# Hybrid RWKV-7 / GLA / SSD stack on one core: more output columns open at once at the head of a layer, and a new pace table for the modulation loads

## The chip, the cores and the metric

One Trainium2 chip, one of its cores. The metric is the device time of one execution of the whole program in microseconds (us), the median over runs. Smaller is better.

## The reference

Four layers on a sequence of 256 tokens of width 2048, batch 1, in float32: layer 0 is RWKV-7, layer 1 is GLA, layer 2 is SSD, layer 3 is RWKV-7 again. Each layer does

```python
mod = jnp.einsum('bd,de->be', c_act, ada_w[i]) + ada_b[i]
shift, scale, gate = jnp.split(mod[:, None, :], 3, axis=-1)
h = rms_normalize(x, norm_g[i], NORM_EPS) * (1 + scale) + shift
...
x = x + (gate * out).astype(x.dtype)
```

Here `ada_w[i]` is 2048 by 6144, and one token vector `c` is multiplied with it: this is the modulation. `out` is the mixer. RWKV mixes h with its shifted copy in six ways, projects four of them (r, k, v, g; 2048 by 2048 each) and two more onto 96 columns (the low-rank inputs of decay and iclr), runs a recurrence over 32 heads, and projects back. GLA projects to q, k (1024 each), v, g (2048 each) and 16 columns `low` for its gate, and runs 4 heads. SSD projects to z and xs (4096 each), B and C (1024 each) and 64 columns dt, with a convolution over xs, B and C, and runs 8 groups.

## The kernel before

**Tiling.** Activations lie as 16 tiles of 128 features by 256 tokens. A weight block is 4 such feature tiles by 256 columns, one load of 512 KB into a `raw` buffer (pool `wpool`, 6 buffers of [128, 1024]). `split` (L334 to L342) makes of it a high part `H` on ScalarE (L338) and the rest `L` on VectorE (L340), 3 buffers each. `prods` (L387) multiplies every feature tile with it as H times high, H times low, L times high: 24 matmuls at L393 for one block. The activations are split likewise by `parts` (L408, L409; with a bias L411, L412), and `xs`, a pool of 16 tiles, holds one layer input.

**jobs and proj.** `jobs` (L359) takes a list of 256-column jobs, opens one PSUM bank for each (two are in the pool `acc`, further ones are passed as `banks`), and goes block by block of four feature tiles over all open jobs. `proj` (L351) calls it with one job at a time. At the head of GLA three jobs are open (`low`, and two of v of head 0), at the head of the last RWKV layer two blocks of v, at the head of SSD dt alone. Layer 0 has its own loop with six blocks of v open, and the change leaves that alone.

**Inputs made on the way.** In GLA and SSD `norm_parts` (L496) makes tile k of h when a job first asks for it: two instructions on VectorE (L504, L412) and one on ScalarE (L411). In RWKV `mixed` (L548) makes tile k of a mix: ScalarE L551 and L408, VectorE L554 and L409; in front of the v mix stands the norm itself, L542 on VectorE. `low` (in `_rwkv`) does 8 feature tiles of a low-rank input: 8 mixes into the pool `xl` (4 buffers), one split, 24 matmuls of 96 columns.

**Modulation.** The gate of layer 0 and the three thirds of layers 1 to 3 come from `ada_third` (L290): 320 steps, each one load of 512 KB into `raw` (L298) and one VectorE instruction of 128 by 1024 (L304, `adaacc`; the first of 16 is on ScalarE). They are spread over the projections: after each block `tick` (L395) counts one tick and runs as many steps as the table `PACE` says, at most two. A layer's shift and scale must be there when it begins; what is missing is run at once by `ada_need`. `hold` stops the ticks from the last output block of a layer until its caller clears it behind the first `jobs` of the next layer; held steps are caught up two a tick.

**Order.** The queue of each engine is put in order by the framework's scheduler, from its own estimate of time. At run time each engine works its queue in that order. All weight and modulation loads go through SP's queue.

**Between two layers** the norm of the new x is a chain: matmuls of the squares (L454), a copy (L468), small matmuls (L471), twelve small VectorE instructions (L1041 to L1049, reciprocal square root), two at L480, a matmul (L483), a copy (L485), and then the first tile of the next layer's input.

Of the kernel before, what the change touches and what calls it, by code (L numbers as in the profile page):

```python
# [15 lines left out]
P = 128  # L16
# [79 lines left out]
PACE = ((0, 60, 78, 150, 319, 530, 660), (0, 0, 16, 96, 234, 292, 320))  # L96
# [33 lines left out]
class Kern:  # L130
# [51 lines left out]
    def bank(self):  # L182
        return self.mx.tile([P, 512], F32, name="mx")
# [159 lines left out]
    def load_w(self, wv, k0, kc, n0, nc_, pad):  # L343
        raw = self.wpool.tile([P, RAWC], F32, name="raw")
        rv = raw[:, 0:kc * pad].rearrange("p (k n) -> p k n", k=kc)
        if pad > nc_:
            self.nc.vector.memset(rv[:, :, nc_:], 0.0)
        self.nc.sync.dma_start(out=rv[:, :, 0:nc_], in_=wv(k0, kc, n0, nc_))
        return raw
# [9 lines left out]
    def jobs(self, wv, jobs, xs, k0=0, banks=()):  # L359
# [6 lines left out]
        for kb in range(0, kt, kc):  # L366
            kn = min(kc, kt - kb)
            for bank, (n0, ncols, evac, pad, tokens) in zip(banks, jobs):
# [15 lines left out]
                if last:  # L384
                    evac(0, bank[:, 0:nj])

# [140 lines left out]
    def _rwkv(self, i, j):  # L527
# [50 lines left out]
        with self.tc.tile_pool(name=f"lp{i}", bufs=1) as lp, ExitStack() as ctx:  # L578
# [13 lines left out]
            if i == self.layers[0]:  # L592

                banks = [self.acc.tile([P, 2, T], F32, name="acc") for _ in range(2)]
                banks += [pv().rearrange("p (j t) -> p j t", j=2) for _ in range(4)]
# [20 lines left out]
            else:  # L616
                sk = scaled(0, DT)
                xs = Lazy(DT, lambda k: mixed(2, next(sk)))
                self.jobs(win, [(2 * D + g * T, T, lambda jj, ps, g=g: keep_v(2 * g, ps), T, False) for g in range(2)], xs)
                g0 = 2  # L620
                self.hold = False
            for g in range(g0, 8):
                self.proj(win, 2 * D + g * T, T, xs, lambda jj, ps, g=g: keep_v(2 * g, ps))
                if i != self.layers[0] and g <= g0 + 3:
                    m, half = divmod(g - g0, 2)
                    low(m, *lw[m], range(8 * half, 8 * half + 8))
# [432 lines left out]
    def _gla(self, i, ctx):  # L1059
        nc = self.nc  # L1060
        A = self.A
        gk = self.gk
        C, NCH = 64, 4
        hs = self.norm_parts(i)
        win = Weights((0, T, A["gla_w_in"][0]), (6144, 16, A["gla_low"][0]))
        wout = Weights((0, T, A["gla_w_out"][0]))

        bc = gk.tile([P, 8, T], F32, name="bcum")
        self.gu = ctx.enter_context(self.tc.tile_pool(name=f"gu{i}", bufs=2))
        first = self.gu.tile([P, 2, 512], F32, name="vt")  # L1070
        self.gla_decay(win, hs, bc, first)
        self.paired(4, lambda h, due: self.gla_head(h, hs, win, bc, due, None if h else first), wout, i)
# [8 lines left out]
    def gla_decay(self, win, hs, bc, vt):  # L1081
# [5 lines left out]
        self.jobs(win, [first] + self.gla_v(0, vt), hs, banks=[self.b1().rearrange("p (j t) -> p j t", j=2)])  # L1087
        self.hold = False
# [148 lines left out]
    def _ssd(self, i):  # L1237
# [13 lines left out]
        self.proj(win, 10240, 64, hs, evdt, pad=P)  # L1251
        self.hold = False
# [22 lines left out]
        self.paired(8, lambda g, due: self.ssd_group(g, hs, win, acd, tk, due), wout, i)  # L1275
# [13 lines left out]
    def ssd_group(self, g, hs, win, acd, tk, due):  # L1289
# [4 lines left out]
        bcx = su.tile([P, 2, T], F32, name="bc")  # L1294

        def conv_evac(t0, dst, step=1):
            def ev(j, ps):
                cp = su.tile([P, 2, T + 3], F32, name="cvp")
                nc.vector.memset(cp[:, :, 0:3], 0.0)
                nc.scalar.copy(out=cp[:, :, 3:], in_=ps)  # L1300
                for u in range(2):
                    self.conv(t0 + j + u * step, cp[:, u, :], dst[:, j + u, :])
            return ev
        self.proj(win, 8192 + T * g, T, hs, conv_evac(32 + g, bcx, 8))
# [37 lines left out]
        xT = su.tile([P, 4, T], F32, name="xT")  # L1342
        self.proj(win, 4096 + 512 * g, 512, hs, conv_evac(4 * g, xT))
# [128 lines left out]
```

## Time and profile before

| what | value |
|---|---|
| runs of the kernel | 2889.27 us median of 3 (2874.83 to 2891.78) |
| the profiled execution | 2887.0 us, its span 2885.0 us |
| mean granted TensorE clock | 0.952 |
| TensorE busy | 2686.2 us, 93% of the span |
| VectorE busy | 2212.4 us, 77% |
| ScalarE busy | 1392.8 us, 48% |
| GpSimd busy | 154.6 us, 5% |

The span is the time from the first to the last instruction; the execution's own time lies 2 us above it. Busy shares are means over stages with different limits. The stages in time, cut where the last column block of each projection is copied out: layer 0 v to 208, k to 360, r to 505, g to 691, out to 872; GLA to about 1345; SSD to about 2128; layer 3 v to 2250, k to 2412, r to 2547, g to 2714, out to 2866.

### The profile page before, as it was taken

Reading aid. Unit: us, or ns where it says so; the run is one execution under the profiler, and the core shown is the slowest. Engines: PE = TensorE matmul, PEld = TensorE weight load, DVE = VectorE, ACT = ScalarE, POOL = GpSimd, SP = SyncE. Lnnn points to the kernel's source line nnn. Section 1 sums busy time; section 2 is a strip of 40 time slices with the busy share of each in tenths; the row PEclk is TensorE's granted clock in tenths of the full one; section 3 lists DMA queues with packets and bytes.
Section 4 is the critical chain, followed back from the end, with each engine's and each line's share of the span. In section 5 each row is a group of like instructions: output and inputs, shape, how many; then the busy total and the mean of one; then the engine's idle time right before and its main releaser. Section 6 shows DMA issues by size and latency. Waiting matters only on the chain.

```text
span 2885.0 us, 64064 instructions
## 1 busy us (share of the span) xinstructions
PE 2686.2 (93%) x26098; PEld 2505.1 (87%) x26098; DVE 2212.4 (77%) x3918; ACT 1392.8 (48%) x2315; POOL 154.6 (5%) x298
## 2 busy tenths in 40 slices
PE   6899999999987899988998999999889999999997
PEld 4789889887877899987988999999879988988887
DVE  5778777877788888877898788887668897666666
ACT  3475655433335454434544454554457756453333
POOL 0011110101000000000000000000000111010100
PEclk8899999999998999999999999999989999999999
DMA  9866557977677888976784767776557665585543
GB/s 348 308 231 190 176 161 261 347 266 278 207 261 244 293 285 291 324 268 197 277 294 161 242 219 228 224 226 216 167 171 236 230 208 190 178 297 194 207 132 108
DMA packets 239126, 673.68 MB, mean 234 GB/s; under 512 B 72272, under 2 KB 78416, under 8 KB 235760
## 3 DMA queue, kind: packets, MB, share of 16 engines
q1 hardware_dynamic: 217904, 580.84, 60.2%
q0 software_dynamic: 20928, 88.75, 8.5%
q8 instruction: 205, 3.36, 0.5%
q14 instruction: 89, 0.73, 0.1%
HBM read 620.66 MB, written 48.82 MB: 232 GB/s over the span
## 4 chain that ended last, share of the span: by engine, by line
PE 66%; DVE 8%; DMA 8%; issue 3%; ACT 2%; SPq 1%; POOL 0%; DVEq 0%; ACTq 0%; POOLq 0%
PE acc L393 53%; DMA raw<-in_ada_w 3%; DVE L L340 2%; PE g L785 2%; DVE adaacc L304 1%; ACT H L338 1%; PE b L897 1%; DMA raw<-in_gla_w_in 1%; DMA dx<-bd 1%; DMA raw<-in_rwkv_w_in 1%; PE b L866 1%; DMA raw<-in_rwkv_w_out 1%; PE b L873 1%; DMA sp<-yd 1%; PE b L1030 1%
## 5 line engine op out<-in xcount | busy, mean ns | idle before, releaser
L393 PE MATMUL acc<-xs,H 128*128 128x256 f32 x8480 | 1634.4, 291 | 36.5 <-ACT H L338 8.1
L393 PEld LDWEIGHTS acc<-xs,H 128*128 128x128 f32 x8480 | 1362.8, 196 | 69.3 <-ACT H L338 11.4
L393 PE MATMUL acc<-xs,L 128*128 128x256 f32 x4240 | 1230.6, 291 | 17.1 <-DVE L L340 16.2
L338 ACT CAST H<-raw 128x1024 fp32r<-128x1024 f32 (+1 forms) x706 | 718.0, 1018 | 854.9 <-PE acc L393 634.3
L340 DVE TENSOR_TENSOR L<-raw,H 128x1024 fp32r<-128x1024 f32 (+1 forms) x706 | 833.7, 1183 | 248.9 <-ACT H L338 234.0
L393 PEld LDWEIGHTS acc<-xs,L 128*128 128x128 f32 x4240 | 830.8, 196 | 31.1 <-DVE L L340 21.5
L304 DVE SCALAR_TENSOR_TENSOR adaacc<-raw,cact,adaacc 128x1024 f32<-128x1024 f32 x300 | 384.0, 1280 | 132.6 <-DMA raw<-in_ada_w 130.2
L393 PE MATMUL acc<-ys,H 128*128 128x256 f32 x1536 | 293.3, 291 | 12.2 <-DVE ys L409 4.9
L393 PEld LDWEIGHTS acc<-ys,H 128*128 128x128 f32 x1536 | 245.9, 195 | 22.0 <-issue 6.6
L393 PE MATMUL acc<-ys,L 128*128 128x256 f32 x768 | 222.1, 290 | 0.4 <-DVE L L340 0.4
L393 PEld LDWEIGHTS acc<-ys,L 128*128 128x128 f32 x768 | 149.6, 195 | 4.6 <-issue 3.6
L551 ACT ACTIVATE hn<-x,mod,omu 128x256 f32<-128x256 f32 x192 | 113.4, 599 | 1.5 <-DVE x L542 1.2
L431 DVE SCALAR_TENSOR_TENSOR x<-acc,mod,x 128x256 f32<-128x256 f32 x192 | 83.6, 477 | 35.7 <-PE acc L393 35.3
L393 PE MATMUL acc<-H,xs 128*128 128x256 f32 x512 | 97.1, 290 | 1.6 <-ACT vt L1078 1.6
L554 DVE SCALAR_TENSOR_TENSOR xm<-x,par,hn 128x256 f32<-128x256 f32 x192 | 88.6, 476 | 1.4 <-ACT hn L551 0.3
L393 PEld LDWEIGHTS acc<-H,xs 128*128 128x128 f32 x512 | 82.4, 197 | 3.1 <-ACT vt L1078 1.8
L393 PE MATMUL acc<-L,xs 128*128 128x256 f32 x256 | 73.8, 289 | 0.0
L785 PE MATMUL g<-abkp 64*128 64x128 f32 x768 | 65.8, 293 | 4.0 <-DVE G L823 2.7
L408 ACT CAST xs<-xm 128x256 fp32r<-128x256 f32 x128 | 50.9, 400 | 35.4 <-DVE xm L554 33.0
L785 PEld LDWEIGHTS g<-abkp 64*128 64x128 f32 x768 | 52.2, 190 | 15.8 <-issue 8.8
L1284 DVE SCALAR_TENSOR_TENSOR cva<-cvp,hcw,cva 128x256 f32<-128x256 f32 x144 | 64.9, 476 | 0.0
L278 DVE SCALAR_TENSOR_TENSOR adaacc<-raw,cact,adaacc 128x512 f32<-128x512 f32 x56 | 41.9, 748 | 27.5 <-DMA raw<-in_ada_w 23.0
(358 smaller groups left out, 3063.0 us busy)
## 6 DMA issues: line engine op xcount, KB each, us to landing
raw<-in_ada_w SPq DMA_DIRECT2D x384, 512.0 KB, 4.8
raw<-in_rwkv_w_in SPq DMA_DIRECT2D x256, 512.0 KB, 4.7
raw<-in_ssd_w_in SPq DMA_DIRECT2D x128, 512.0 KB, 4.4
raw<-in_gla_w_in SPq DMA_DIRECT2D x96, 512.0 KB, 5.2
raw<-in_ssd_w_out SPq DMA_DIRECT2D x64, 512.0 KB, 4.2
raw<-in_rwkv_w_out SPq DMA_DIRECT2D x48, 512.0 KB, 4.2
abkp<-kd POOLq DMA_DIRECT2D x16, 1024.0 KB, 7.3
raw<-in_gla_w_out SPq DMA_DIRECT2D x32, 512.0 KB, 4.9
```

What stands on the lines that cost most here:

```text
L278: nc.vector.scalar_tensor_tensor(out=acc, in0=raw[:, u, :], scalar=self.cact[:, k:k + 1], in1=acc, op0=ALU.mult, op1=ALU.add)
L304: nc.vector.scalar_tensor_tensor(out=acc, in0=raw, scalar=self.cact[:, k:k + 1], in1=acc, op0=ALU.mult, op1=ALU.add)
L338: nc.scalar.copy(out=hi, in_=raw[:, a:a + n])
L340: nc.vector.tensor_tensor(out=lo, in0=raw[:, a:a + n], in1=hi, op=ALU.subtract)
L393: self.nc.tensor.matmul(ps, lhs, rhs, start=first and part == 0 and w is hi, stop=last and w is lo)
L408: nc.scalar.copy(out=t[:, 0, :], in_=src)
L431: nc.vector.scalar_tensor_tensor(out=self.x[:, t, 1:], in0=ps[:, u, :], scalar=gate[:, t:t + 1], in1=self.x[:, t, 1:], op0=ALU.mult, op1=A ...
L551: nc.scalar.activation(t1, x[:, k, 1:], AF.Identity, scale=self.omu[:, col:col + 1], bias=self.mods[(i, 0)][:, k:k + 1])
L554: done[k] = nc.vector.scalar_tensor_tensor(out=xm, in0=x[:, k, 0:T], scalar=self.p("rwkv_mu", col), in1=t1, op0=ALU.mult, op1=ALU.add)
L785: self.nc.tensor.matmul(ps[h][:, n * C:(n + 1) * C], s[r, q, c * C:(c + 1) * C], t[r, q, c * C:(c + 1) * C], start=True, stop=True)
L866: nc.tensor.matmul(ps[r, n * H:(n + 1) * H], G[h][:, q, r], tk[:, 2, q, HS[h]], start=not c, stop=not c or h == 1)
L1284: nc.vector.scalar_tensor_tensor(out=a, in0=src[:, k:k + T], scalar=w[k], in1=a, op0=ALU.mult, op1=ALU.add)
```

## The change

Three things. (1) The head of a layer opens more columns in its first `jobs`: in the last RWKV layer six blocks of v instead of two, in GLA `low` and the v of heads 0 and 1 instead of head 0 alone, in SSD dt together with B and C and the two xs blocks of group 0. The low-rank inputs of layer 3, one half behind each of the third to the sixth block of v before, now stand two halves behind each of the seventh and the eighth. `go=True` clears `hold` behind the first four feature tiles instead of behind the whole call. dt, padded to 128 columns, now comes in four loads and not two. (2) The zeroes of a padded block are written by GpSimd and not by VectorE. (3) The table PACE is replaced.

```diff
-PACE = ((0, 60, 78, 150, 319, 530, 660), (0, 0, 16, 96, 234, 292, 320))
+PACE = ((0, 57, 134, 272, 496, 620), (0, 36, 98, 194, 290, 320))
...
-            self.nc.vector.memset(rv[:, :, nc_:], 0.0)
+            self.nc.gpsimd.memset(rv[:, :, nc_:], 0.0)
...
+            if go:
+                self.hold = False
+
+    def pairs(self, bank, n):
+
+        return [bank().rearrange("p (j t) -> p j t", j=2) for _ in range(n)]
...
-                self.jobs(win, [(2 * D + g * T, T, lambda jj, ps, g=g: keep_v(2 * g, ps), T, False) for g in range(2)], xs)
-                g0 = 2
-                self.hold = False
+                self.jobs(win, [(2 * D + g * T, T, lambda jj, ps, g=g: keep_v(2 * g, ps), T, False) for g in range(6)], xs,
+                          banks=self.pairs(pv, 4), go=True)
+                g0 = 6
             for g in range(g0, 8):
                 self.proj(win, 2 * D + g * T, T, xs, lambda jj, ps, g=g: keep_v(2 * g, ps))
-                if i != self.layers[0] and g <= g0 + 3:
-                    m, half = divmod(g - g0, 2)
-                    low(m, *lw[m], range(8 * half, 8 * half + 8))
+                if i != self.layers[0]:
+                    for k in (0, 8):
+                        low(g - g0, *lw[g - g0], range(k, k + 8))
...
-        self.jobs(win, [first] + self.gla_v(0, vt), hs, banks=[self.b1().rearrange("p (j t) -> p j t", j=2)])
-        self.hold = False
+        self.jobs(win, [first] + self.gla_v(0, vts[0]) + self.gla_v(1, vts[1]), hs, banks=self.pairs(self.b1, 3), go=True)
...
-        self.proj(win, 10240, 64, hs, evdt, pad=P)
-        self.hold = False
+
+        first = su.tile([P, 2, T], F32, name="bc"), su.tile([P, 4, T], F32, name="xT")
+        cb, cx = self.conv_evac(32, first[0], 8), self.conv_evac(0, first[1])
+        self.jobs(win, [(10240, 64, evdt, P, False), (8192, T, cb, T, False), (4096, T, cx, T, False),
+                        (4096 + T, T, lambda _, ps: cx(2, ps), T, False)], hs, banks=self.pairs(self.b1, 2), go=True)
```

How it moves the queues, at three places. First VectorE between layer 0 and GLA, in the norm's chain (`rsv`, `rst`, `rsr` are its small tiles, `adaacc` a modulation step, `L` a split). Before:

```order
L1041 TENSOR_SCALAR rsv<-nb 128x2
L304 SCALAR_TENSOR_TENSOR adaacc<-raw,cact,adaacc 128x1024
L1042 TENSOR_SCALAR rst<-rsv 128x2
L304 SCALAR_TENSOR_TENSOR adaacc<-raw,cact,adaacc 128x1024
L347 MEMSET raw 128x4x112
L1044 TENSOR_SCALAR rsr<-rst 128x2
L304 SCALAR_TENSOR_TENSOR adaacc<-raw,cact,adaacc 128x1024
L1047 TENSOR_TENSOR rst<-rsr 128x2
L340 TENSOR_TENSOR L<-raw,H 128x512
L304 SCALAR_TENSOR_TENSOR adaacc<-raw,cact,adaacc 128x1024
L1048 SCALAR_TENSOR_TENSOR rst<-rst,rsv 128x2
```

VectorE at the same place in the changed kernel:

```order
L1048 TENSOR_SCALAR rsv<-nb 128x2
L304 SCALAR_TENSOR_TENSOR adaacc<-raw,cact,adaacc 128x1024
L1049 TENSOR_SCALAR rst<-rsv 128x2
L1051 TENSOR_SCALAR rsr<-rst 128x2
L1054 TENSOR_TENSOR rst<-rsr 128x2
L1055 SCALAR_TENSOR_TENSOR rst<-rst,rsv 128x2
L1056 SCALAR_TENSOR_TENSOR rsr<-rst,rsr 128x2
L1054 TENSOR_TENSOR rst<-rsr 128x2
L1055 SCALAR_TENSOR_TENSOR rst<-rst,rsv 128x2
L1056 SCALAR_TENSOR_TENSOR rsr<-rst,rsr 128x2
L304 SCALAR_TENSOR_TENSOR adaacc<-raw,cact,adaacc 128x1024
L1054 TENSOR_TENSOR rst<-rsr 128x2
```

Between `rsv` and L480 stood five steps of the modulation, three splits and three memsets before; now three steps and nothing else.

Second VectorE in the k projection of layer 0, in the first unit (`thd`, `abk`, `n` are tiles of the RWKV unit, `xs` and `xm` of the mix). Before:

```order
L340 TENSOR_TENSOR L<-raw,H 128x1024 x2
L752 TENSOR_TENSOR thd<-thd,abk 128x512
L754 SCALAR_TENSOR_TENSOR abk<-abk 128x512
L340 TENSOR_TENSOR L<-raw,H 128x1024
L756 SCALAR_TENSOR_TENSOR abk<-abk,bkk 128x256
L758 SCALAR_TENSOR_TENSOR abk<-abk,nkk,Pt 128x256
```

VectorE at the same place in the changed kernel, from the last mixes on:

```order
L416 TENSOR_TENSOR xs<-xm,xs 128x256
L304 SCALAR_TENSOR_TENSOR adaacc<-raw,cact,adaacc 128x1024
L561 SCALAR_TENSOR_TENSOR xm<-x,par,hn 128x256
L340 TENSOR_TENSOR L<-raw,H 128x1024 x2
L759 TENSOR_TENSOR thd<-thd,abk 128x512
L761 SCALAR_TENSOR_TENSOR abk<-abk 128x512
L304 SCALAR_TENSOR_TENSOR adaacc<-raw,cact,adaacc 128x1024
L340 TENSOR_TENSOR L<-raw,H 128x1024
L763 SCALAR_TENSOR_TENSOR abk<-abk,bkk 128x256
```

Before, no step of the modulation stands in this projection; now there is one about every second split.

Third ScalarE in layer 3, where v ends (`sp<-acc` copies a block of v out, `hn` and `xl` are the mixes of the low-rank inputs, `lo_dec` takes their sum, `xs` is the mix for k). Before:

```order
L408 CAST xl<-xm 128x256
L551 ACTIVATE hn<-x,mod_0_16959,omu 128x256 x2
L338 CAST H<-raw 128x1024
L551 ACTIVATE hn<-x,mod_0_16959,omu 128x256
L338 CAST H<-raw 128x1024
L629 ACTIVATE lo_dec<-pv 96x256
L629 ACTIVATE lo_iclr<-pv 96x256
L338 CAST H<-raw 128x1024
L571 COPY sp<-acc 128x512
L408 CAST xs<-xm 128x256 x2
```

ScalarE from the copy of the last block of v on, in the changed kernel:

```order
L578 COPY sp<-acc 128x512
L415 CAST xl<-xm 128x256
L558 ACTIVATE hn<-x,mod_0_18395,omu 128x256
L415 CAST xl<-xm 128x256
L558 ACTIVATE hn<-x,mod_0_18395,omu 128x256
L338 CAST H<-raw 128x1024
L415 CAST xl<-xm 128x256
```

There the pair of `xl` and `hn` goes on for 16 feature tiles behind that copy, with two splits between, before the first `xs` of k; before, the last `xl` stood four splits ahead of the end of v.

## Rows read from the trace of the kernel before

**Rows 1.** The page, part 1: busy time and share of the span.

```profile
PE 2686.2 (93%) x26098; PEld 2505.1 (87%) x26098; DVE 2212.4 (77%) x3918; ACT 1392.8 (48%) x2315; POOL 154.6 (5%) x298
```

**Rows 2.** Busy time by stage, all engines; columns in the first line.

```profile
core 0: us, PE busy (x) PEld busy (x) DVE busy (x) ACT busy (x) POOL busy (x), PEclk, DMA share, GB/s
208.00:360.00 152.00, 145.74 (x1656) 137.99 (x1655) 121.57 (x271) 97.84 (x196) 18.15 (x33) 0.94 0.59 186
505.00:691.00 186.00, 179.06 (x1926) 160.36 (x1927) 141.71 (x231) 64.85 (x102) 20.85 (x39) 0.96 0.83 294
691.00:872.00 181.00, 158.88 (x1496) 139.64 (x1492) 144.60 (x250) 59.40 (x104) 10.94 (x21) 0.94 0.74 252
910.00:1303.00 393.00, 376.21 (x2994) 354.74 (x2993) 318.96 (x402) 183.64 (x264) 0.00 (x0) 0.97 0.83 292
1358.00:1512.00 154.00, 141.70 (x1118) 136.62 (x1118) 138.54 (x242) 82.69 (x126) 2.19 (x4) 0.94 0.78 270
1600.00:2110.00 510.00, 500.84 (x4181) 486.88 (x4181) 400.90 (x705) 247.73 (x352) 5.21 (x8) 0.99 0.67 217
2136.00:2250.00 114.00, 110.43 (x872) 109.50 (x873) 99.44 (x170) 86.63 (x158) 8.77 (x20) 0.94 0.68 219
2547.00:2714.00 167.00, 167.00 (x1955) 151.90 (x1955) 103.58 (x189) 61.20 (x97) 20.02 (x38) 1.00 0.66 230
2714.00:2866.00 152.00, 149.00 (x1536) 134.87 (x1533) 104.30 (x213) 56.51 (x97) 11.78 (x22) 0.99 0.44 141
```

**Rows 3.** Line L304 alone by stage: us, VectorE busy (count), PEclk, DMA share, GB/s.

```profile
505.00:691.00 186.00, 40.03 (x32) 0.96 0.83 294
691.00:872.00 181.00, 49.97 (x40) 0.94 0.74 252
910.00:1303.00 393.00, 126.71 (x99) 0.97 0.83 292
2547.00:2714.00 167.00, 5.10 (x4) 1.00 0.66 230
2714.00:2866.00 152.00, 0.00 (x0) 0.99 0.44 141
```

**Rows 4.** PE in order of time at the three changes of layer: start, us, instruction [idle before].

```profile
872.34 0.61 PE L471 MATMUL nb<-cst,hn 128*128 128x1 f32 x4 [0.46 <-ACT hn L468]
...
887.08 1.22 PE L483 MATMUL nb<-xm,cst 128*128 128x256 f32 x2 [1.52 <-DVE xm L480]
...
1348.47 0.61 PE L471 MATMUL b<-cst,hn 128*128 128x1 f32 x4 [0.41 <-ACT hn L468]
1356.11 1.22 PE L483 MATMUL b<-xm,cst 128*128 128x256 f32 x2 [7.02 <-DVE xm L480]
...
2128.42 0.61 PE L471 MATMUL b<-cst,hn 128*128 128x1 f32 x4 [0.46 <-ACT hn L468]
2132.05 1.19 PE L483 MATMUL b<-xm,cst 128*128 128x256 f32 x2 [3.02 <-DVE xm L480]
```

**Rows 5.** The chain that ended last: one long unbroken piece of matmuls.

```profile
1582.87 68.46 PE acc L393 x569
```

**Rows 6.** Groups by line: busy us, mean ns | idle before, released by.

```profile
L338 ACT CAST H<-raw 128x1024 fp32r<-128x1024 f32 (+1 forms) x706 | 718.0, 1018 | 854.9 <-PE acc L393 634.3 <-issue 65.4 <-DMA raw<-in_rwkv_w_in 30.0
L304 DVE SCALAR_TENSOR_TENSOR adaacc<-raw,cact,adaacc 128x1024 f32<-128x1024 f32 x300 | 384.0, 1280 | 132.6 <-DMA raw<-in_ada_w 130.2 <-ACT adaacc L302 0.6 <-DVE sT L1170 0.3
L551 ACT ACTIVATE hn<-x,mod,omu 128x256 f32<-128x256 f32 x192 | 113.4, 599 | 1.5 <-DVE x L542 1.2
L408 ACT CAST xl<-xm 128x256 fp32r<-128x256 f32 x64 | 25.1, 399 | 13.4 <-DVE xm L554 13.4
L1001 POOL MEMSET Tt<- 128x1024 f32 x16 | 15.4, 961 | 88.8 <-DMA td<-Tt 79.0 <-DVE xm L554 6.0 <-DVE abk L760 3.9
```

**Rows 7.** Line L347: the memset of a padded block, durations min/median/max.

```profile
L347 DVE MEMSET raw<- x6: 432/432/485, 875.9 to 1325.8; 128x448 f32 x4, 128x512 f32 x2
```

More of the change, by code (lines that the diff above doesn't have):

```diff
@@ L357, in proj, with jobs @@
             self.jobs(wv, [(n0 + a, w, lambda j, ps, a=a: evac(a // P + j, ps), pad or w, tokens)], xs, k0)
-    def jobs(self, wv, jobs, xs, k0=0, banks=()):
+    def jobs(self, wv, jobs, xs, k0=0, banks=(), go=False):
         kt = len(xs)
@@ L594, in _rwkv @@
                 banks = [self.acc.tile([P, 2, T], F32, name="acc") for _ in range(2)]
-                banks += [pv().rearrange("p (j t) -> p j t", j=2) for _ in range(4)]
+                banks += self.pairs(pv, 4)
                 xs = []
@@ L1069, in _gla @@
         self.gu = ctx.enter_context(self.tc.tile_pool(name=f"gu{i}", bufs=2))
-        first = self.gu.tile([P, 2, 512], F32, name="vt")
+        first = [self.gu.tile([P, 2, 512], F32, name="vt") for _ in range(2)]
         self.gla_decay(win, hs, bc, first)
-        self.paired(4, lambda h, due: self.gla_head(h, hs, win, bc, due, None if h else first), wout, i)
+        self.paired(4, lambda h, due: self.gla_head(h, hs, win, bc, due, first[h] if h < 2 else None), wout, i)
     def gla_v(self, h, vt):
@@ L1079, in gla_v, with gla_decay @@
         return [block(0), block(1)]
[L1081 removed]
+    def gla_decay(self, win, hs, bc, vts):
         nc = self.nc
@@ L1274, in _ssd @@
         nc.scalar.copy(out=tk.rearrange("p a h -> p (a h)"), in_=ps[:, 0:4 * NH])
-        self.paired(8, lambda g, due: self.ssd_group(g, hs, win, acd, tk, due), wout, i)
+        self.paired(8, lambda g, due: self.ssd_group(g, hs, win, acd, tk, due, None if g else first), wout, i)
     def conv(self, t, src, dst):
@@ L1287, in conv, with conv_evac, ev, ssd_group @@
         nc.vector.scalar_tensor_tensor(out=dst, in0=th, scalar=1.0, in1=a, op0=ALU.add, op1=ALU.mult)
-    def ssd_group(self, g, hs, win, acd, tk, due):
+    def conv_evac(self, t0, dst, step=1):
+        nc = self.nc
+        def ev(j, ps):
+            cp = self.su.tile([P, 2, T + 3], F32, name="cvp")
+            nc.vector.memset(cp[:, :, 0:3], 0.0)
+            nc.scalar.copy(out=cp[:, :, 3:], in_=ps)
+            for u in range(2):
+                self.conv(t0 + j + u * step, cp[:, u, :], dst[:, j + u, :])
+        return ev
+    def ssd_group(self, g, hs, win, acd, tk, due, first):
         nc = self.nc
@@ L1293, in ssd_group @@
         HG = slice(8 * g, 8 * g + 8)
[L1294 to L1304, printed above, removed]
+        if first:
+            bcx, xT = first
+        else:
+            bcx, xT = su.tile([P, 2, T], F32, name="bc"), su.tile([P, 4, T], F32, name="xT")
+            self.proj(win, 8192 + T * g, T, hs, self.conv_evac(32 + g, bcx, 8))
         Bt, Ct = bcx[:, 0, :], bcx[:, 1, :]
@@ L1340, in ssd_group @@
         nc.scalar.activation(de, de, AF.Exp)
-        xT = su.tile([P, 4, T], F32, name="xT")
-        self.proj(win, 4096 + 512 * g, 512, hs, conv_evac(4 * g, xT))
+        if not first:
+            self.proj(win, 4096 + 512 * g, 512, hs, self.conv_evac(4 * g, xT))
         xc = []
```

## The prediction

> **What bounds the kernel now.** I read the page first [rows 1]: TensorE is busy 2686 of 2885 us and VectorE 2212, so at most 199 us of TensorE's idle time can be had, and VectorE has little room in any stage where the mean is exceeded. Then the busy time by stage [rows 2], because a mean over four kinds of layer decides nothing. The reader is to see there that the two long matrix stages are near TensorE's limit (GLA 376 of 393 us, late SSD 501 of 510), while the first RWKV layer is not: its last stage, 691 to 872 us, keeps TensorE busy 159 of 181 us, and the same stage of layer 3 149 of 152. Third, the modulation steps in the same stretches [rows 3]: layer 0 carries 32 and 40 of them in its g and out stages, layer 3 four and none. Fourth, the three changes of layer in order of time [rows 4]. Last the prices [rows 5 to 7].
>
> A matmul costs 68.46 / 569 = 0.1203 us in an unbroken piece [rows 5], a modulation step 1.28 us of VectorE, and VectorE also stood idle 130.2 us in front of the 300 steps until their load had landed, 0.43 us each [rows 6].
>
> **Where the steps go.** VectorE's order has 706 splits in the old kernel, two more in the new, and they serve as milestones; I count the L304 steps between the same milestones. Layer 0 up to the 80th split (the end of v, and k): 0 before, 29 now. To the 112th (r): 18, now 23. To the 160th (g and most of out): 47, now 37. To the 176th (end of out and the change of layer): 23, now 8. GLA (to the 304th): 105, now 84. The first two groups of SSD (to the 352nd): 35, now 20. The rest of SSD (to the 528th): 45, now 75. Layer 3: 27, now 23. Both sums are 300: the table moves the steps and removes none. So the change is mostly a question of where a step is cheap.
>
> **The change, part by part.**
>
> 1. *Changes of layer.* From L471 to L483 PE waits for the small VectorE chain: 14.74 us between layers 0 and 1, 7.64 between 1 and 2, 3.63 between 2 and 3 [rows 4]. The last has nothing else in the chain and is the floor. The new order leaves three steps in the first, one in the second, one in the third: 3.63 + 3 x 1.28 = 7.5, 4.9 and 4.9. That is -7.3, -2.7 and +1.3, together **-8.7**. Ends: -15 if the steps slip out of the way (both long waits at the floor), -2 if each of the five also waits three times the mean of 0.43 us for its load.
>
> 2. *Six blocks of v in layer 3, the head.* From 2136 to 2250 us there are 872 matmuls, 104.9 us at full pace, in 114 [rows 2, 5]. The granted clock of 0.94 means about 12% of the stretch at 1.2 instead of 2.4 GHz, some 7 us of the 9 lost; that clock was low because PE had waited in the change of layer, and that wait stays. Opening more columns saves the micro-waits for the inputs and some of the later cold time: **-4**, ends -9 and 0. For GLA and SSD I book nothing for the columns as such: in the old trace the scheduler already mixes several jobs' matmuls, and GLA's loss is spread thinly (17 us of 393).
>
> 3. *The same, the tail.* The low-rank inputs now come last. Behind the copy of the last block of v, ScalarE has 16 pairs of `hn` and `xl` to do, 16 x (0.599 + 0.399) = 16 us, and two splits, at most 1.02 us each [rows 6]. PE has 48 matmuls for it, 5.8 us. k's first input is queued behind them. Some 12 us of PE are uncovered, a little of it filled from the scheduler's other work: **+10**, ends 0 and +18. This is the wait that takes the place of the old head.
>
> 4. *k and r of layer 0.* 29 + 5 = 34 more steps. For the price of a step inside an RWKV layer I compare the g and out stages of layers 0 and 3, which do the same work: 186 + 181 - 167 - 152 = 48 us longer for 72 - 4 = 68 more steps [rows 2, 3], 0.70 us each. So **+23.8**. Lower end 0: VectorE is idle 30 us of the 152 in k, which could take most of 29 x 1.28 = 37 us. Upper end 34 x (1.28 + 0.43) = 58, if each step and its wait for the load go on the path. I stay at 0.70, the only row that prices a step where it stands among the same neighbours; the DMA queues have room here (share 0.59), VectorE has not.
>
> 5. *g and out of layer 0.* 10 + 15 fewer steps, of which three fall inside the wait of part 1: 22 x 0.70 = **-15.4**, ends -30 (as dear as a bare step) and 0.
>
> 6. *GLA.* 21 fewer. TensorE's whole idle time there is 16.8 us over 99 steps [rows 2, 3], 0.17 us each at most: **-3.6**, ends -17 and 0.
>
> 7. *SSD.* 15 fewer at the head, where VectorE is at 138.5 of 154 us and PE loses 12 [rows 2]: **-5**, ends -12 and 0. The head itself is not shorter in work: up to the first use of M the order has 548 large matmuls and 10 steps, 551 and 13 before. 30 more in the rest, where PE loses 9 us of 510: 30 x 0.17 = **+5.1**, ends 0 and +21 (at 0.70).
>
> 8. *Rest of layer 3.* 4 x 0.70 = **-2.8**, ends -5 and 0.
>
> 9. *Memsets on GpSimd, dt in four loads.* Six memsets of 0.43 us leave VectorE [rows 7]; three lie in the wait of part 1 and are counted there. On GpSimd a memset of 1024 columns takes 0.96 us [rows 6], so 448 columns take between 0.4 and 1.0, ahead of a load that is issued while PE still works on the layer before: 0, ends -1 and +4 if each of the four comes late.
>
> Sum: -8.7 - 4 + 10 + 23.8 - 15.4 - 3.6 - 5 + 5.1 - 2.8 = -0.6. The profiled execution took 2887.0 us, its span 2885.0 and 2 us around it; 2887.0 - 0.6 = 2886.4. The median of the runs, 2889.27, is 2.3 us higher, well inside their spread of 17 us. I write 2886.
>
> **The rivals.**
>
> *A. The steps are covered in k.* For it: k has DMA share 0.59 against 0.83 in g, TensorE is busy 146 of 152 us although VectorE is idle 30, and ScalarE's tail in layer 3 may be filled with k's work. Against it: 29 steps are 37 us, more than VectorE's idle time there. With parts 3 and 4 at nothing the sum is -0.6 - 33.8 = -34.4, or 2853 us.
>
> *B. k of layer 0 becomes bound by VectorE: slower.* The place is 208 to 360 us. VectorE does its queue in order, so a step that waits for its load holds the splits behind it, and SP's queue, through which these loads now come, also carries the small transfers of the triangular inverse. It decides from the point where VectorE's work there passes the stage's length: 121.6 + 1.28 n = 152, n = 24 steps, against up to 29 that now stand between the end of v and the start of r. Its price is part 4 at 58 us: -0.6 + 34.2 = +33.6, or 2921 us. Against it: VectorE's idle time absorbs the first steps, and layer 3's k carries a few steps without such a loss.
>
> *C. The loads were hidden anyway.* Then part 5 gives nothing, since what slowed layer 0's out stage was its own small transfers and not the steps: -0.6 + 15.4 = +14.8, or 2902 us. For it: the out stage's DMA share is 0.74, not full. Against it: 22 us of idle TensorE there and 3 in layer 3. The Trainium skill, HBM Reference, section Specifications (TRN2), says a core that streams alone gets about 425 GB/s; by that the 252 to 294 GB/s of g and out [rows 2] leave room, thinning the loads relieves no queue, and the sum would be C's. The trace's own sign against it is the busy share of 0.83 at 294 GB/s, so this mix of transfers would fill the queues near 294 / 0.83 = 354 GB/s.
>
> *That the change does not do what it says* holds for half of it: in GLA and SSD the opened columns meet a scheduler that had mixed the jobs already, which is why part 2 prices layer 3 alone. It moves no time of its own.
>
> **How the numbers follow.** Forecast 0.48, A 0.22, B 0.17, C 0.13. About 1% (29 us, 2860 to 2918) is what a measurement of this kernel can tell from no change. A lies beyond it on one side, and with a share of it and a tail of the forecast I give 0.20 to faster. B lies just beyond it on the other: half of B and a tail from part 3, SSD's later groups and C give 0.16 to slower. The rest, 0.64, is within 1%. The range runs from A to B, 2850 to 2920. The likeliest case alone: 2870 to 2902, from parts 1 to 3 and 7 at half their ends.
>
> **What would show it.** After the change: PE from L471 to L483 near 7.5 us at the first change of layer (right if under 9, wrong if over 12). No L304 row in k before, some 20 to 29 now, and k (end of v to the last copy of k, 152 us) longer by 10 to 25 us; if it stays within 5, A is right, if it grows by 40, B. Out of layer 0 (181 us) shorter by 10 or more; if not, C. At the end of v in layer 3 a gap of PE of about 10 us for ScalarE's `xl`. Early SSD (154 us) shorter by about 5. The forecast is wrong as a whole if the stage table moves by more than 10 us in GLA or late SSD, for which it has no mechanism.

## The result and the profile after

The changed kernel takes 2958.89 us (median of 4 runs, 2956.85 to 2963.64) against 2882.72 for the kernel before on the same chip: a ratio of 1.0265, 95% interval 1.0232 to 1.0297. It is slower by some 76 us; the forecast was no change. A ratio here is always that of a kernel's runs to runs of the kernel before, and an interval is the 95% interval of that ratio.

The page and the group of L304, beside [rows 1] and [rows 6]:

```profile
span 2955.1 us, 64020 instructions
...
PE 2703.4 (91%) x26098; PEld 2511.4 (85%) x26098; DVE 2209.5 (75%) x3914; ACT 1398.6 (47%) x2317; POOL 157.4 (5%) x306
...
L304 DVE SCALAR_TENSOR_TENSOR adaacc<-raw,cact,adaacc 128x1024 f32<-128x1024 f32 x300 | 384.2, 1281 | 260.0 <-DMA raw<-in_ada_w 255.3
```

VectorE does the same 300 steps in the same 384 us. What grew is the time in which it stood in front of them: 130.2 us before, 255.3 now. Busy shares cannot show that; VectorE's even fell.

Stages between the same last copies as before (us, from the profiled executions). Beside the changed kernel stand the runs in which one part was made alone in the kernel before; the last line is the ratio of all runs.

| stage | before | after | table alone | GLA head alone | SSD head alone | v of layer 3 alone | memsets alone |
|---|---|---|---|---|---|---|---|
| layer 0 | 872.9 | 875.4 | 873.8 | 868.1 | 864.8 | 873.1 | 869.0 |
| GLA | 476.1 | 475.8 | 460.4 | 489.9 | 476.4 | 473.6 | 473.2 |
| SSD | 779.9 | 826.9 | 813.7 | 784.7 | 780.0 | 782.6 | 775.1 |
| layer 3 v | 121.7 | 112.7 | 123.8 | 122.7 | 124.8 | 113.3 | 122.5 |
| layer 3 k | 162.3 | 182.5 | 161.8 | 163.9 | 163.3 | 194.0 | 158.9 |
| layer 3 r, g, out | 456.6 | 466.6 | 455.6 | 453.9 | 471.7 | 460.1 | 454.4 |
| ratio | 1 | 1.0265 | 1.0119 | 1.0042 | 1.0073 | 1.0115 | 0.9964 |

Read it along the lines: the 70 us between the two profiles are 47 in SSD and 21 in layer 3. Read it down: four parts cost, each at a place of its own, one gains, and their sum (+3.1%) is near the whole (+2.65%). How far a stage moves by itself is seen in layer 0: eight kernels with the old table work it in the order of before, and it took 862.3 to 873.1 us in their profiles. So a difference under 10 us in one stage of one profile is weak evidence.

In SSD the parts do not add up. The new PACE costs it 34 us alone, but 54 with the rest of the change beside it (772.9 to 826.9, the run with the old table below). What makes the 20 us between was not taken apart.

The stages of after that answer to [rows 2], columns as there:

```profile
209.00:364.00 155.00, 143.64 (x1536) 134.34 (x1535) 135.99 (x265) 92.61 (x179) 14.81 (x27) 0.96 0.73 242
514.00:676.00 162.00, 154.54 (x1739) 141.71 (x1737) 117.02 (x169) 59.76 (x93) 17.79 (x33) 0.97 0.83 301
676.00:875.00 199.00, 178.27 (x1886) 156.84 (x1887) 151.47 (x295) 67.56 (x118) 14.87 (x28) 0.97 0.63 211
1604.00:2160.00 556.00, 512.37 (x4164) 492.05 (x4164) 423.28 (x725) 248.39 (x352) 5.19 (x8) 0.97 0.65 218
2293.00:2476.00 183.00, 165.47 (x1723) 150.69 (x1723) 155.16 (x341) 120.37 (x246) 22.23 (x45) 0.90 0.59 189
```

k of layer 0 took 21 steps in its stretch where there had been none, and 155 us instead of 153. Late SSD, with 61 steps instead of 40, needs 556 us for what took 510, and PE is idle for 44 us of it instead of 9.

VectorE's longest wait in late SSD, after (line, what it waited for: us, times, longest):

```profile
DVE adaacc L304 <- DMA raw<-in_ada_w: 84.3, 45, 3.8
```

The same in the kernel before, 1600 to 2110 us:

```profile
DVE adaacc L304 <- DMA raw<-in_ada_w: 36.5, 30, 2.7
```

And PE's there, after; the first row was 0.4 us before:

```profile
PE acc L400 <- DVE L L340: 15.1, 15, 2.6
PE acc L400 <- DVE ys L416: 10.9, 3, 5.6
```

One such wait in order of time, VectorE in the changed kernel:

```profile
1901.61 1.21 DVE L340 TENSOR_TENSOR L<-raw,H 128x1024 fp32r<-128x1024 f32 x1
1902.75 0.68 DVE L1368 TENSOR_TENSOR xd<-xc,de 128x512 f32<-128x512 f32 x1
1905.22 1.28 DVE L304 SCALAR_TENSOR_TENSOR adaacc<-raw,cact,adaacc 128x1024 f32<-128x1024 f32 x1 [1.79 <-DMA raw<-in_ada_w]
1906.42 2.35 DVE L340 TENSOR_TENSOR L<-raw,H 128x1024 fp32r<-128x1024 f32 x2
```

SP's queue beside it:

```profile
1900.52 0.33 SPq L298 DMA_DIRECT2D raw<-in_ada_w  x1
1902.85 4.01 SPq L348 DMA_DIRECT2D raw<-in_ssd_w_in  x2
```

The load of the step goes out at 1900.52 and the step starts at 1905.22, 4.7 us later, as soon as it has landed; over SSD's 94 steps the median from issue to step is also 4.7 us. Behind the step stand two splits that PE needs. The Trainium skill, Trainium Kernel Development and Optimization, section Best Practices, says that for engines other than TensorE occupancy is a fine measure of how near the limit they are; by VectorE's 646 busy of 827 us in SSD (78%) it would have room left, and the experiments below do not agree.

PE at the changes of layer, after, beside [rows 4]:

```profile
874.78 0.61 PE L478 MATMUL nb<-cst,hn 128*128 128x1 f32 x4 [0.46 <-ACT hn L475]
883.42 1.19 PE L490 MATMUL nb<-xm,cst 128*128 128x256 f32 x2 [8.04 <-DVE xm L487]
1350.13 1.02 PE L478 MATMUL b<-cst,hn 128*128 128x1 f32 x4 [0.46 <-ACT hn L475]
1355.78 1.22 PE L490 MATMUL b<-xm,cst 128*128 128x256 f32 x2 [4.63 <-DVE xm L487]
2177.48 0.61 PE L478 MATMUL b<-cst,hn 128*128 128x1 f32 x4 [0.46 <-ACT hn L475]
2183.55 1.19 PE L490 MATMUL b<-xm,cst 128*128 128x256 f32 x2 [5.46 <-DVE xm L487]
```

Start to start 8.6, 5.7 and 6.1 us, where 7.5, 4.9 and 4.9 were forecast.

The v stage of layer 3, before and after (columns as in [rows 2]):

```profile
2129.03:2250.73 121.70, 112.53 (x880) 110.91 (x881) 103.89 (x188) 89.41 (x164) 8.77 (x20) 0.93 0.65 210
```

```profile
2178.09:2290.81 112.72, 103.37 (x830) 100.79 (x830) 80.92 (x138) 67.88 (x113) 3.81 (x7) 0.95 0.63 205
```

It is 9.0 us shorter, but TensorE is idle in it for as long as before, 9.2 and 9.3 us. It does 50 matmuls fewer, because 48 of the 96 of the low-rank inputs now stand behind its end, in k.

The end of v in layer 3, ScalarE in order of time, after:

```profile
2290.24 0.58 ACT L578 COPY sp<-acc 128x512 f32<-128x512 f32 x1
2290.71 0.41 ACT L415 CAST xl<-xm 128x256 fp32r<-128x256 f32 x1
2291.02 0.60 ACT L558 ACTIVATE hn<-x,mod,omu 128x256 f32<-128x256 f32 x1
...
2299.88 0.41 ACT L415 CAST xl<-xm 128x256 fp32r<-128x256 f32 x1 [1.58 <-DVE xm L561]
...
2308.26 0.40 ACT L415 CAST xl<-xm 128x256 fp32r<-128x256 f32 x1
2308.57 0.60 ACT L558 ACTIVATE hn<-x,mod,omu 128x256 f32<-128x256 f32 x1
2309.07 0.39 ACT L415 CAST xs<-xm 128x256 fp32r<-128x256 f32 x1
```

The first `xs` of k comes 18.8 us behind the last copy of v. All engines in these 25 us, after (columns as in [rows 2]):

```profile
2291.00:2316.00 25.00, 18.59 (x61) 12.94 (x62) 22.23 (x47) 21.29 (x49) 5.53 (x14) 0.55 0.43 142
```

And in the 25 us behind the same copy before:

```profile
2251.00:2276.00 25.00, 24.49 (x198) 23.32 (x197) 19.99 (x35) 19.27 (x39) 1.85 (x3) 1.00 0.62 206
```

61 matmuls instead of 198, ScalarE and VectorE busy for 21 and 22 of the 25 us, and the granted clock at 0.55. The chain that ended last also holds a modulation step there:

```profile
2294.64 3.43 DMA raw<-in_ada_w
2298.09 1.28 DVE adaacc L304
2301.04 0.60 ACT hn L558
```

### The profile page after: what moved, and what is told of

It reads as the page before. It is cut to its first block, busy times and chain, and to the rows that moved or that the text cites. A ratio compares the mean times of both kernels' runs of the same rounds, so it can differ in the third digit from the quotient of the medians.

```text
span 2955.1 us, 64020 instructions
## 1 busy us (share of the span) xinstructions
PE 2703.4 (91%) x26098; PEld 2511.4 (85%) x26098; DVE 2209.5 (75%) x3914; ACT 1398.6 (47%) x2317; POOL 157.4 (5%) x306
## 4 chain that ended last, share of the span: by engine, by line
PE 61%; DMA 16%; DVE 15%; issue 5%; ACT 2%; SPq 1%; POOL 0%; DVEq 0%; POOLq 0%; ACTq 0%
PE acc L400 45%; DMA raw<-in_ada_w 12%; DVE L L340 5%; PE pv L400 3%; DVE adaacc L304 2%; PE b L400 2%; PE g L792 1%; DMA raw<-in_rwkv_w_in 1%; DMA sp<-yd 1%; ACT H L338 1%; PE b L904 1%; DMA dx<-bd 1%; DVE dt L965 1%; DMA bd<-LT 1%; PE b L873 0%
## 5 line engine op out<-in xcount | busy, mean ns | idle before, releaser
L400 PE MATMUL acc<-xs,H 128*128 128x256 f32 x8128 | 1567.3, 291 | 34.3 <-ACT xs L415 10.9
L400 PEld LDWEIGHTS acc<-xs,H 128*128 128x128 f32 x8128 | 1305.7, 196 | 66.3 <-issue 18.5
L400 PE MATMUL acc<-xs,L 128*128 128x256 f32 x4064 | 1182.0, 292 | 35.6 <-DVE L L340 33.4
L338 ACT CAST H<-raw 128x1024 fp32r<-128x1024 f32 (+2 forms) x708 | 718.4, 1015 | 834.5 <-PE acc L400 650.6
L340 DVE TENSOR_TENSOR L<-raw,H 128x1024 fp32r<-128x1024 f32 (+2 forms) x708 | 831.8, 1179 | 206.9 <-ACT H L338 191.3
L400 PEld LDWEIGHTS acc<-xs,L 128*128 128x128 f32 x4064 | 795.3, 196 | 53.3 <-DVE L L340 41.4
L304 DVE SCALAR_TENSOR_TENSOR adaacc<-raw,cact,adaacc 128x1024 f32<-128x1024 f32 x300 | 384.2, 1281 | 260.0 <-DMA raw<-in_ada_w 255.3
L400 PEld LDWEIGHTS acc<-ys,H 128*128 128x128 f32 x1536 | 248.5, 198 | 37.2 <-DVE ys L416 11.7
L400 PE MATMUL pv<-xs,H 128*128 128x256 f32 x512 | 102.7, 299 | 8.0 <-ACT H L338 5.4
L400 PEld LDWEIGHTS pv<-xs,H 128*128 128x128 f32 x512 | 86.4, 206 | 10.7 <-ACT H L338 6.2
L400 PE MATMUL pv<-xs,L 128*128 128x256 f32 x256 | 76.0, 298 | 2.0 <-DVE L L340 2.0
L400 PE MATMUL acc<-H,xs 128*128 128x256 f32 x384 | 69.6, 283 | 0.0
```

The source lines that it names most:

```text
L304: nc.vector.scalar_tensor_tensor(out=acc, in0=raw, scalar=self.cact[:, k:k + 1], in1=acc, op0=ALU.mult, op1=ALU.add)
L338: nc.scalar.copy(out=hi, in_=raw[:, a:a + n])
L340: nc.vector.tensor_tensor(out=lo, in0=raw[:, a:a + n], in1=hi, op=ALU.subtract)
L400: self.nc.tensor.matmul(ps, lhs, rhs, start=first and part == 0 and w is hi, stop=last and w is lo)
```

## The experiments

**The parts against each other.** The table alone in the kernel before:

```diff
-PACE = ((0, 60, 78, 150, 319, 530, 660), (0, 0, 16, 96, 234, 292, 320))
+PACE = ((0, 57, 134, 272, 496, 620), (0, 36, 98, 194, 290, 320))
```

> The kernel before with the new pace table and nothing else. Pace theory: of the 76 us, some 45 arise in the late SSD stage (1600 to 2110 us before, 510 us long, 555 after), because the table puts 30 more modulation steps there and VectorE, which works in order, waits for the load of each (84.3 us of such waits there after, 36.5 before). It expects about 2882.7 + 45 = 2928 us and that stage near 555 us. Column theory (the rival): the six-block head of layer 3 and the wider heads of GLA and SSD made it, and the table only rearranges; it expects within 10 us of 2883 and a late SSD stage near 510 us.

2909.92 us, 1.0119 (1.0084 to 1.0154). GLA gained 15.7 us, and SSD lost 33.8 for 92 steps instead of 77. Per step added on balance that is 2.25 us, but the table does two things there. In front of the 352nd split, counted as in the prediction, it takes 14 steps out, and the stretch from the 304th became 7.3 us shorter (181.2 to 173.9); from there to the 528th it puts 30 in, and that stretch became 42.7 us longer (590.7 to 633.4). A step added late in SSD cost 1.4 us here. So the table alone makes SSD slower, and its gain in GLA hides half of that.

The old table in the changed kernel:

> The changed kernel with the old pace table. Pace theory: the late SSD stage falls back to about 510 us, the loss of some 24 us around the end of v in layer 3 stays: 2959 - 45 = 2914 us. Column theory: within 10 us of 2959. If the two parts only hurt together (the table loads SSD and the column change delays what follows), below 2895.

2932.65 us, 1.0189. SSD was back at 772.9, but k of layer 3 took 199.2. Against this kernel the changed one has 29 steps more between the same two points (the 354th and the 530th split here, since two more stand ahead of them) and takes 62.7 us longer from one to the other (572.5 to 635.2): 2.2 us a step. Layer 3's v as before, new table kept:

```diff
-                self.jobs(win, [(2 * D + g * T, T, lambda jj, ps, g=g: keep_v(2 * g, ps), T, False) for g in range(6)], xs,
-                          banks=self.pairs(pv, 4), go=True)
-                g0 = 6
+                self.jobs(win, [(2 * D + g * T, T, lambda jj, ps, g=g: keep_v(2 * g, ps), T, False) for g in range(2)], xs)
+                g0 = 2
+                self.hold = False
...
-                if i != self.layers[0]:
-                    for k in (0, 8):
-                        low(g - g0, *lw[g - g0], range(k, k + 8))
+                if i != self.layers[0] and g <= g0 + 3:
+                    m, half = divmod(g - g0, 2)
+                    low(m, *lw[m], range(8 * half, 8 * half + 8))
```

> The changed kernel with layer 3's v as before (two blocks open, low-rank inputs behind the third to the sixth block), new table kept. Tail theory: the low-rank inputs bunched behind the last block of v cost the 24 us that arise between the 13200th and the 13600th large matmul; it expects 2959 - 24 = 2935 us, and the late SSD stage still near 555. Rival: that loss is of the steps that the table put there or of the clock, and stays: 2950 to 2960 us.

2944.80 us, 1.0236: 14 us back, not 24; v and k together fell from 295.2 to 277.8, but r rose to 152.4. Both undone:

> The changed kernel with both undone: old table and layer 3's v as before; left are the wider heads of GLA and SSD, the zeroes on GpSimd and dt in four loads. Pace and tail theory together: what is left is worth little, 2875 to 2895 us. Column theory in its part for GLA and SSD: 2900 us or more.

2907.51 us, 1.0102 (1.0054 to 1.0149): a miss for the pace and tail theory, and the time that the column theory gave. What is left costs 27 us. But 10 of them lie in GLA, and 24 in layer 3, whose code was that of before. Neither theory had named layer 3, so the heads were run alone.

> The kernel before with GLA's wider head alone (low and the v of two heads open, hold cleared behind the first four feature tiles). With the old table and the old v of layer 3, the kernel with both wider heads took 27 us more than before: 10 in GLA, 6 less in SSD, 24 more in layer 3, whose code was that of before. Head theory: GLA's head costs those 10 us in GLA, where the span grew at the 5200th to 5600th large matmul, and nothing after: 2890 us. Rival (the order of the queues in layer 3 follows from anything that shifts the steps' ticks): the 24 us of layer 3 appear here also: 2910 us.

2891.95 us, 1.0042 (1.0020 to 1.0064): 13.7 us in GLA, nothing in layer 3. As the head theory said. TensorE there stood 11.7 us in front of VectorE's results between 1005 and 1090 us (a split 4.3, `rsr` 4.2, `ke` and `kn` 3.2), where the kernel before has no such wait from 1008 to 1075; what makes VectorE late was not taken apart.

> The kernel before with SSD's wider head alone (dt, B and C, two xs blocks open; dt in four loads, which makes two more ticks). Head theory: 6 us less in SSD and nothing elsewhere: 2874 us. Rival: the two more ticks shift every later modulation step, layer 3's r and g among them, and the 24 us of layer 3 are here: 2898 us.

2899.58 us, 1.0073 (1.0046 to 1.0100): the rival. SSD gained nothing; r, g and out of layer 3 took 471.7 us instead of 456.6. With the count of ticks set back by two:

```diff
+        self.tk -= 2
```

> The kernel before with SSD's wider head, and the count of ticks set back by the two that dt's two further loads add. Tick theory: r, g and out of layer 3 grew from 457 to 472 us with SSD's head alone because later modulation steps stand two ticks earlier there; set back, they are 457 again and the whole 2880 us. Rival: the scheduler writes another order for layer 3 for other reasons; they stay near 472 us and the whole near 2897.

2887.53 us, 1.0031 (1.0007 to 1.0054), r, g and out 456.9. From k of layer 3 on, all queues held the same instructions in the same order as before. So SSD's head costs mainly through two ticks: they shift the later steps, and the scheduler writes another order for layer 3. What in that order costs 15 us stays open; VectorE's waits for `dx` and for modulation loads in k and r were 30 to 36 us in the four profiles with the old order or the table alone, and 41 to 53 in seven with another order, but 32 in the changed kernel.

The new v alone, and the memsets alone:

> The kernel before with the new v of layer 3 alone (six blocks open, the low-rank inputs behind the seventh and the eighth), old table, old heads in GLA and SSD. Up to the end of SSD it is the kernel before, and its stages are to stay within 3 us. Tail theory: v gains 9 us (121.7 to about 113), k loses 20 or more (162.3 to above 182), since ScalarE has the low-rank inputs to make while PE stands: the whole 2882 + 14 to 2882 + 25, 2896 to 2907 us. Rival (the new v cost 14 and 25 us in the other kernels only because SSD's head had shifted layer 3's order): the whole within 5 us of 2882.

2910.74 us, 1.0115 (1.0096 to 1.0134), above the range given: v -8.4, k +31.7. As in the changed kernel, most of what v gains is work that has moved: 818 matmuls lie in it instead of 880, and TensorE is idle in it for 11.0 us instead of 9.2. The tail costs nearly four times what v gains.

> The kernel before with the six memsets on GpSimd alone. By the stages nothing hangs on them: within 5 us of 2882. Rival: they move the order of the queues like the two ticks of SSD's head did, and layer 3's r, g and out take 470 us instead of 457: 2895 us.

2869.53 us, 0.9964 (0.9947 to 0.9981), below the range given: faster than both kernels, by about 10 us against before, and the version to keep. The two profiles lie 16.6 us apart. Some 8 of these arise between the end of GLA and the head of SSD, where two of the six stood in VectorE's queue [rows 7], and 4 in layer 0, ahead of all six. That 0.43 us each grow to this is not shown, since the order of the queues in SSD and from v to g of layer 3 is another too.

**What makes the tail.** The low-rank inputs ahead of blocks 7 and 8 instead of behind:

```diff
-                self.proj(win, 2 * D + g * T, T, xs, lambda jj, ps, g=g: keep_v(2 * g, ps))
                 if i != self.layers[0]:
                     for k in (0, 8):
                         low(g - g0, *lw[g - g0], range(k, k + 8))
+                self.proj(win, 2 * D + g * T, T, xs, lambda jj, ps, g=g: keep_v(2 * g, ps))
```

> The changed kernel with the two low-rank inputs of layer 3 ahead of its seventh and eighth block of v, instead of behind them; nothing else is moved. Tail theory: the low-rank input behind the last block is what k waits for, the k stage of layer 3 (182.5 us after, 162.3 before) falls to about 165 and the whole to 2959 - 17 = 2942 us. Rival: k is long because VectorE and ScalarE have too much work there in any order (the 32 mixes have moved next to k's 16): the k stage stays above 177 us, the whole within 5 us of 2959.

2957.52 us: the whole stayed. k fell to 170.1, but v rose to 125.4, together 295.5 as before it: the loss only moved ahead. Four blocks open, one half behind each of the last four:

> The changed kernel with four blocks of v open in layer 3 instead of six, and the halves of the low-rank inputs behind the fifth to the eighth block, one behind each. Bunching theory: low-rank inputs two halves at a time cost ScalarE and VectorE more than PE has work beside them, wherever they stand (the kernel with them ahead of blocks 7 and 8 had v and k together at 295.5 us, the one with them behind at 295.2, before 284.0); spread again, v and k together fall to 284 us or less and the whole to 2959 - 12 = 2947 us. Rival: it is the open blocks and the steps beside them; v and k stay at 293 us or more.

2953.49 us. v and k fell to 278.3, 6 below the kernel before, and v took 112.5 with 14 matmuls fewer than before (1.7 us) and 5.9 us of TensorE idle instead of 9.2. So the loss in v and k comes from the bunching, and four open columns, with the inputs spread, do save waits. But r rose to 156.8, and 5 us are left of it.

**Work or wait in SSD.** Two attempts did not settle it. Loads issued one step ahead:

> The changed kernel, in which each modulation load is issued one step ahead of the VectorE instruction that reads it (the same loads, the same instructions, one raw buffer held longer). Wait theory: late SSD is long because VectorE, in order, waits for each step's load (84.3 us in 61 steps); those waits go, the SSD stage falls from 827 us to about 790, and the whole to about 2959 - 45 = 2914 us or less, since GLA and layer 0 have such waits too. Work theory: VectorE's own 1.28 us a step make it, the waits only move to other places: SSD stays at 815 us or more, the whole at 2945 us or more. If the buffer held longer makes the weight loads late: above 2965 us.

2965.23 us. The median from issue to step in SSD was 4.8 us, unchanged; that the scheduler and the six buffers put the loads where they had been is a reading of this, not shown. Two own buffers for the modulation (`name="adaraw", bufs=2`, `wpool` with 4):

> The changed kernel in which the modulation loads have two buffers of their own and the weight blocks keep four (six in all, as before, since the memory is full). Buffer theory: in SSD a modulation load is issued a median of 4.7 us ahead of the instruction that reads it, as long as it takes to land, because its buffer is the one that was just freed, and the next weight load waits for that same buffer in its turn; with buffers of their own the lead grows to the distance between steps (6 us or more), VectorE's waits for these loads (255 us after) fall below 120 us, SSD from 827 to below 800, the whole to 2930 us or less. Work theory: VectorE's 1.28 us a step decide, the waits move to other lines, SSD stays above 815 us. If four weight buffers are too few, PE waits for L and H more everywhere, and the whole lies above 2970 us.

3003.27 us. The lead grew to 6.0 us and the waits in SSD fell to 20 us, but the scheduler drew 20 steps out of SSD and 22 out of layer 3 into layer 0, and v and out of layer 0 took 39 and 57 us more than in the changed kernel. ScalarE's waits for weight loads in layer 0 grew from 42 to 69 us; what of the loss is of the four weight buffers and what of the moved steps was not separated. So one of the two was taken away instead, in the 96 steps of SSD's time. Both kernels leave that part of the modulation out. The first keeps the loads (`late` is true for these steps):

```diff
-                    nc.vector.scalar_tensor_tensor(out=acc, in0=raw, scalar=self.cact[:, k:k + 1], in1=acc,
-                                                   op0=ALU.mult, op1=ALU.add)
+                    w = 16 if late else RAWC
+                    nc.vector.scalar_tensor_tensor(out=acc[:, 0:w], in0=raw[:, 0:w], scalar=self.cact[:, k:k + 1],
+                                                   in1=acc[:, 0:w], op0=ALU.mult, op1=ALU.add)
```

> The changed kernel in which the 96 modulation steps of SSD's time (the gate of layer 2, shift and scale of layer 3) keep their loads, but VectorE's instruction reads 16 columns instead of 1024; that part of the modulation is left out of the computation. Wait theory: what costs is that VectorE stands before a step until its load has landed; the load is still there, so SSD stays above 800 us (827 after) and L304 still waits some 100 us there. Work theory: 94 x (1.28 - 0.1) = 111 us of VectorE's work are gone, and SSD falls below 785 us.

2889.20 us. VectorE's wait in SSD, and behind it the stage as a whole (columns as in [rows 2]):

```profile
DVE adaacc L306 <- DMA raw<-in_ada_w: 98.2, 60, 4.0
```

```profile
1354.00:2118.00 764.00, 735.68 (x6090) 709.40 (x6090) 563.84 (x1145) 378.76 (x553) 11.20 (x19) 0.98 0.70 239
```

The second keeps VectorE's instruction, which reads the sum tile itself, and loads nothing:

> The changed kernel in which the same 96 steps keep VectorE's instruction in full, but it reads the sum tile itself, and nothing is loaded; that part of the modulation is left out of the computation. Wait theory: SSD falls to 785 us or less, though VectorE has the same work. Work theory: SSD stays above 810 us. If both this and the kernel with loads alone fall by about half (to some 800), it is the sum of both.

2927.18 us, the same two rows of this kernel, and VectorE's longest wait there:

```profile
DVE adaacc L308 <- DMA raw<-in_ada_w: 8.4, 5, 2.4
DVE L L344 <- ACT H L342: 86.2, 77, 2.9
```

```profile
1353.00:2142.00 789.00, 744.44 (x6094) 715.56 (x6093) 639.08 (x1138) 379.75 (x553) 11.22 (x19) 0.97 0.52 175
```

The changed kernel, with 827 us and 646 of VectorE busy in SSD:

```profile
DVE adaacc L304 <- DMA raw<-in_ada_w: 103.4, 61, 3.8
DVE L L340 <- ACT H L338: 31.9, 31, 2.9
```

Taking 83 us of work away gives 63, taking 95 us of waits (and 7 of work) 39. SSD came to 764 us without the work, where the work theory had said below 785, and to 788 without the loads, where the wait theory had said 785 or less. Each theory denied the other's run, so neither holds alone: VectorE's work and its waits for the loads cost together, and either one taken away undoes most or all of the 47 us. Two limits. Without the loads VectorE waited 54 us longer for ScalarE's `H`, so a wait for a load that goes is in part replaced by another. And the second kernel has 85 steps in SSD instead of 94, the rest having gone to GLA, and no traffic of those loads (DMA share 0.52 instead of 0.66), which was not tested by itself. In the changed kernel VectorE is held by a step for 1.28 + 103.4 / 94 = 2.4 us in the mean.

**A better table?** The new one for layer 0, GLA filled up, the old one from tick 319:

```diff
+PACE = ((0, 57, 134, 319, 530, 660), (0, 36, 98, 234, 292, 320))
```

> The kernel before with a mixed table: the new one to tick 134 (layer 0), the old one's points from tick 319 on, so that the steps which the new table puts into late SSD stand in GLA. Stage theory (a step costs about 1.8 us in SSD, 0.3 in GLA, next to nothing in the k and r of layer 0): GLA gains about 10 us over before, SSD stays at 780, the whole 2870 us. Rival (the layer's length follows from VectorE's total work, wherever the steps stand): within 5 us of 2880.

2897.88 us, 1.0051 (1.0032 to 1.0071). In its profiled execution, one of its shortest, GLA gained 10.7 and SSD stayed, as the prices said, and r of layer 3 lost 14.8. The same with the new table to tick 272:

> The kernel before with a table that follows the new one to tick 272 (the end of GLA) and the old one from tick 319 on: the steps go where the stages show them cheap, and late SSD is as before. Stage theory: GLA gains 10 to 15 us as in the two kernels with fewer steps there, SSD and layer 0 stay, 2865 to 2870 us. Against it stands that layer 3's queues come out in another order than before (as the order shows): in seven of the eight other kernels where they did, its k, r, g and out together took 5 to 60 us more than before, which would leave 2880 us or more.

2891.72 us, 1.0033 (1.0013 to 1.0052): GLA -13.8, layer 0 +9, r of layer 3 +11.9. None of the three new tables beat the old one. Nor does another order always cost: of the seven kernels with the old v and another order in layer 3, k, r, g and out together took 5 to 21 us more in five, and 2 and 6 us less in two (the table alone, the memsets alone).

## Why the prediction was wrong

1. *Changes of layer*, -8.7: -6.1, -2.0 and +2.4, together -5.7. Right, within its ends.
2. *Head of v*, -4 with an end at -9: -9.0, and -8.1 to -11.3 in the other kernels with the columns open and no low-rank input ahead of them. That the figure lies inside the range is luck. Of the 9.0, 50 matmuls less are 6.0 us at 0.1203, and the rest goes with the clock (0.95 instead of 0.93); the waits that the term was to save did not get shorter (9.2 and 9.3 us). The forecast booked the moved matmuls in neither part.
3. *Tail of v*, +10 with an end at +18: +20.2, and +31.7 alone. The mechanism was the one named, at the place named: TensorE is idle for 18.3 us of k instead of 9.8. The size missed three things that the rows show: the 48 matmuls that came over from v, 5.8 us; a modulation load inside the chain; and the clock at 0.55 behind the gap.
4. *k and r of layer 0*, +23.8: +2.6 and +5.2, for 27 more steps in the trace and not 34 (six more stand in v). The price of 0.70 us was wrong for k; rival A saw this part as it came. The count of steps behind it also has a slip: its numbers for the new kernel add up to 299, not 300.
5. *g and out of layer 0*, -15.4: -23.3 and +17.3, so -6.0, for 19 fewer steps by the trace and not 25 (28 and 25 instead of 32 and 40 in the stretches of [rows 3]). The price came from comparing layers 0 and 3, whose stages also differ in the order of their queues. Order alone moves more between g and out than that: in layer 3 g took 167.2 us and out 155.3 before, 188.9 and 132.9 with SSD's head alone. The result is nearer to rival C, which gave this part nothing.
6. *GLA*, -3.6: -0.4. The figure is near by luck: the table alone gives -15.7 and the wider head alone, which had been booked at nothing, +13.7.
7. *SSD*, -5 and +5.1: **+47.0. This is the step that failed.** I took 30 x 0.17 = 5.1, "0.17 us each at most", from TensorE's idle time in GLA shared out over GLA's steps. That is a mean where room is left, not the price of one more. Measured, a step added late in SSD cost 1.4 us with the table alone and 2.2 in the changed kernel, where VectorE is held for 2.4 us by a step. The -5 at the head of SSD was sound: -7.3 with the table alone. Rival B had the mechanism, "a step that waits for its load holds the splits behind it", but put it in k of layer 0, and its condition, that VectorE's work passes the stage's length, did not hold where the loss came: VectorE was busy 423 of 556 us in late SSD. I had its 401 of 510 us in view there and left out the waits. That the table costs SSD 34 us alone and 54 with the rest of the change beside it stays open.
8. *Rest of layer 3*, -2.8: r, g and out +10.0. Not a matter of four steps but, as far as the runs show, of another order, which SSD's two ticks alone bring (+15.1), and which no row of before could show.
9. *Memsets*, 0 with an end at -1: 0.36% less when made alone, some 10 us, beyond that end; the cause stays open.

The forecast had named its own test: wrong as a whole if late SSD moved by more than 10 us. It moved by 46.

## What to carry to other kernels

Price one more instruction on an engine that works its queue in order from the time it holds the engine, its own duration and its wait for data together, and not from the idle time of another engine. Here that was the upper side: 2.4 us held, 1.4 to 2.2 paid. Divide a loss by the steps that were added where it arose, and not by the balance of a longer stretch. Before crediting a stage with a gain, count the work in it: v became 9 us shorter mostly because work had left it. Opening more columns pays only if what is pushed behind them still has work of TensorE beside it. Where a scheduler writes the order, run each part alone: a change of two ticks moved 15 us in a layer that nobody had edited.

## What the runs showed that was not expected

With the same order of instructions from r to out, layer 3 took 456.6 and 456.9 us in two kernels, and 453.9 in a third with a few neighbours swapped; with other orders of the same work it took 454.4 to 478.5. And the gap of PE cost twice here: in the 25 us behind v the granted clock was 0.55 after PE had stood waiting, near the lower of its two levels (1.2 GHz), where the same stretch before stood at 1.00, the higher (2.4).
